# Moving the stores of V, merge gates and gated h to the queues of the engines that make them, V by key and block in DRAM, T blocks on VectorE, and P3 kept in the second quad

## The chip, the cores and the metric

The kernel runs on one core of one Trainium2 chip. The metric is the device time of one execution in microseconds (us). Several runs of a kernel are taken, and their median counts. One more execution is recorded by the hardware profiler; every time of a single instruction, wait or stage below comes from that one, counted from the start of its span.

## The reference, cut to what is computed

One hybrid decoder block, batch 1, 2048 positions, width 1024, float32:

```python
proj = x @ w_in + b_in                      # 1024 -> 9216 columns
q, k, v, g_attn, u_lru, g_lru, gate_logits = split(proj)
q, k = rope(q), rope(k)                     # 3 groups x 8 heads x 64
# group (window, dilation): (128,1), (512,4), (2048,16): causal band attention,
# keys gathered by stride, outputs of the groups weighted by their softmax denominators
attn = merge(dilated_band_attention(q[g], k[g], v[g]) for g in 0, 1, 2)
y_a  = (attn * silu(g_attn)) @ w_attn_proj
u    = causal_depthwise_conv(u_lru)         # width 4
h    = rg_lru(u)                            # gates, then a scan over positions
y_b  = (h * silu(g_lru)) @ w_lru_proj
merged = sigmoid(gate_A) * y_a + sigmoid(gate_B) * y_b
out  = layer_norm(alpha * x + merged @ w_out + b_out)
```

## The kernel before

**Stages.** Stage A (0 to about 1535 us) is the input projection with all that follows elementwise from it; stage B (to about 1900) is attention; stage C1 (to about 2075) merges the groups and projects the LRU branch; stage C2 (to the end) projects the attention branch, merges, projects out and normalises. A float32 product is made of three float32r matmuls: high part times high part, high times low, low times high. So every weight tile and every block of x has a high part (an ACT copy that rounds: `prep_w` L268 for weights, `hi_lo` L220 for x) and a low part (a subtraction: L232 for weights, L221 for x, on VectorE (DVE) or GpSimd (POOL)).

**Stage A.** The positions are in four chunks of 512. A half of the stage takes two chunks; the second half begins at 779.8 us in program order. A *quad* pairs two tiles of 128 output columns with the two chunks of the half and the two halves of the contraction: a 2x2 by 2x2 block product. The first quad of a half computes its 8 block products plainly; the other 35 use a seven-product scheme with the block combinations T1 to T4 of x (in `comb` and `fourth`) and S1 to S4 of the weights (`added`, `sums`). S1 and S3 are made by a DMA that POOL issues and that adds in flight (L250, tile wS). One product is 12 matmuls of 128x512 (L605) into one PSUM bank, and one *tick* of the loop; `evacuate` takes the bank with the seven results kept in part in e, u2 and u3. `MID` and `EDGE` are the orders of the seven products. In the first half the low parts of the weights go to DRAM (L285, `wl_scr`), and the second half loads them back (`load_lo`, L290, tile l, four buffers) in place of computing them; a weight tile comes in 256 KB pieces (L239).

**Chains.** What follows a quad's result is a generator: `qk_chain` (swap of halves by four loads L310, rotary, split, stores L327, L338, L341), `v_chain` (four transposes on PE, ACT copy into the tile vs L366, of which there are two, and the store L370), `mg_chain` (tanh L384, store L390), `silu_chain`, and `lru` (ending with h times its gate on POOL and the store L525 to `hb_scr`). `yield Ask(...)` hands the rest of a chain to a later tick in which the engines named have time left in a budget; `at(tick, fn)` and `later(n, fn)` put work into a fixed tick. The generator only sets the program order of each engine; on the chip each engine runs its own list and waits for semaphores.

**Queues.** SP issues nearly all DMAs; ACT issues the output of attention (L996), the last five stores of `mg_scr` (L386) and the result; POOL issues the accumulating ones. The DMAs of SP and ACT together use eight semaphores in turn (the DMAHW in the order's waits), in program order: each of them waits until the one eight before it has landed. Those of POOL have semaphores of their own (DMASW).

**Attention.** 12 units (`unit_parts`: one head pair of one group, the groups in the order 0, 2, 1) of 16 steps. A unit needs q and k tiles (A from `qh_scr` and `ql_scr` L805, C from `k_scr` L784, split by POOL at L792, L793, L795; L780 and L781 are memsets for the first two units) and the V tile of its group (`v_parts`, L822, L824, L826), which serves four units.

Of the kernel before, what the change touches and what calls it, by code (L numbers as in the profile page):

```python
# [31 lines left out]
def hybrid_block_kernel(ctx: ExitStack, tc: tile.TileContext, a: dict, out: bass.AP):  # L32
# [16 lines left out]
    v_scr = [[dram.tile([S, 260], F32, name=f"v_scr{g}{j}") for j in range(2)] for g in range(3)]  # L49
# [29 lines left out]

    def softplus():  # L80
        lam = lr[:, 7, :]
        t = [cst.tile([P, 8], F32, name=f"spt{i}") for i in range(4)]
        dve.tensor_scalar(out=t[0], in0=lam, scalar1=-1.0, scalar2=None, op0=ALU.mult)
        dve.tensor_tensor(out=t[1], in0=lam, in1=t[0], op=ALU.min)
        act.activation(t[1], t[1], AF.Exp)
        dve.tensor_scalar(out=t[2], in0=t[1], scalar1=2.0, scalar2=None, op0=ALU.add)
        dve.reciprocal(out=t[2], in_=t[2])
        dve.tensor_tensor(out=t[1], in0=t[1], in1=t[2], op=ALU.mult)
        dve.tensor_tensor(out=t[2], in0=t[1], in1=t[1], op=ALU.mult)
        dve.tensor_scalar(out=t[3], in0=t[2], scalar1=1.0 / 17, scalar2=1.0 / 15, op0=ALU.mult, op1=ALU.add)  # L90
        for c in (13, 11, 9, 7, 5, 3, 1):
            dve.tensor_tensor(out=t[3], in0=t[3], in1=t[2], op=ALU.mult)
            dve.tensor_scalar(out=t[3], in0=t[3], scalar1=1.0 / c, scalar2=None, op0=ALU.add)
        dve.tensor_tensor(out=t[3], in0=t[3], in1=t[1], op=ALU.mult)
        dve.tensor_scalar(out=t[0], in0=t[0], scalar1=0.0, scalar2=2.0, op0=ALU.max, op1=ALU.mult)
        dve.scalar_tensor_tensor(out=sp2, in0=t[3], scalar=4.0, in1=t[0], op0=ALU.mult, op1=ALU.add)
# [39 lines left out]
    MID, EDGE = (1, 6, 7, 5, 2, 4, 3), (1, 2, 6, 7, 4, 5, 3)  # L136
# [91 lines left out]
    def drop_raw(b, kk):  # L228
        give(xr.pop((b, kk)))
# [72 lines left out]
    def qk_chain(rw, f, c):  # L302
# [48 lines left out]
    def v_chain(vt, sgn, f, c):  # L351
# [18 lines left out]
        sp.dma_start(dst.rearrange("(b p) f -> p b f", p=P), vs)  # L370
# [8 lines left out]
    def mg_chain(y, sgn, f, c, bank=None):  # L379
# [50 lines left out]
    def lru(i, c, ub):  # L430
# [91 lines left out]
        tt(pool, g, g, h, ALU.mult)  # L522
        give(h)
        yield Ask()
        sp.dma_start(hb_scr[i * P:(i + 1) * P, c * CH:(c + 1) * CH], g)  # L525
# [13 lines left out]
    for h in range(2):  # L539
        for p, (kind, f0, f1) in enumerate(seq):  # L540
            plan.append((h, ((f0, kind), (f1, kind)), None if p == 0 else EDGE if p == len(seq) - 1 else MID, p, kind))
# [74 lines left out]
    def evacuate(s, j):  # L616
# [20 lines left out]
        elif pid == 5:  # L637
            result(s, 1, c1, b, Q["u3"])
            tt(dve, Q["u2"], Q["u2"], b, ALU.add)
        elif pid == 4:  # L640
            result(s, 1, c0, b, Q["u3"])
        else:
            result(s, 0, c1, b, Q["u2"])
        last = {"e": (2, 6), "u2": (3,), "u3": (4, 5)}
        for n, p in last.items():
            if pid in p and all(order.index(x) <= j for x in p):
# [11 lines left out]
    for s in range(1, NQ):  # L658
# [9 lines left out]
        at(t0 - 4, lambda s=s: added(s, "S1", "A22"))  # L668
        at(t0 - 4, lambda s=s: added(s, "S3", "A11"))
# [29 lines left out]
    def comb(kk):  # L699
# [684 lines left out]
```

## Time and profile before

| | us |
|---|---|
| median of 3 runs | 2354.79 (2354.69 to 2357.52) |
| the profiled execution's own time | 2354.13 |
| its span | 2352.4 |
| PE busy in it | 2241.2 (95%) |
| PE waits for a low-part load in it | 26.8, in 17 waits |
| granted TensorE clock, mean | 0.978 |

The span is what the profiler sees from the first instruction to the last; the execution's own time is 1.7 us longer. The rows of the profile are groups of instructions by line, engine, operation and tile (tile<-inputs), with busy time, the mean duration of one in ns, and the idle time just ahead of them with what ended it. "SPq" is SP's DMA queue; a row of waits has total us, times, longest us. The lines follow where they are used.

### The profile page before, as it was taken

How to read it: one execution, taken by the hardware profiler on the slowest of the kernel's cores; microseconds unless marked ns; L12 is line 12 of the kernel's file. 1: busy time of each engine (PE TensorE's matmuls, PEld its weight loads, DVE VectorE, ACT ScalarE, POOL GpSimd, SP SyncE). 2: the span in 40 equal slices, each digit the busy share in tenths (PEclk: the TensorE clock that was granted, in tenths of full speed). 3: DMA queues.
4: the chain of work that ended last, by engine and by line, in shares of the span. 5: the costliest groups of instructions: out<-in, count | busy, mean ns of one | idle time of the engine just before them, and what ended most of it. 6: DMA issues, size and time to landing. Idle time of an engine off the chain costs nothing.

```text
span 2352.4 us, 34614 instructions
## 1 busy us (share of the span) xinstructions
PE 2241.2 (95%) x11008; PEld 1877.7 (80%) x11008; DVE 1717.5 (73%) x3122; ACT 1087.8 (46%) x1977; POOL 1005.6 (43%) x754
## 2 busy tenths in 40 slices
PE   6999999999999799999999999989999999989998
PEld 4788888888788687787787777788999878768886
DVE  6888888899889676666677776545666568747677
ACT  4346445455455455465465665455666611121100
POOL 5554555456445433223232232357676436612220
PEclk8999999999999899999999999999999999999999
DMA  6887997988988998897898888897786688874431
GB/s 238 246 251 238 278 281 224 281 257 264 268 260 294 287 245 240 243 256 228 236 261 242 260 241 253 255 258 181 196 226 161 175 253 295 267 248 157 157 117 63
DMA packets 347175, 551.48 MB, mean 234 GB/s; under 512 B 99057, under 2 KB 140017, under 8 KB 342385
## 3 DMA queue, kind: packets, MB, share of 16 engines
q1 hardware_dynamic: 308160, 489.80, 66.6%
q0 software_dynamic: 20160, 36.71, 9.6%
q10 hardware_dynamic: 18672, 22.75, 3.1%
q8 instruction: 88, 1.44, 0.3%
q14 instruction: 95, 0.77, 0.1%
HBM read 343.81 MB, written 180.16 MB: 223 GB/s over the span
## 4 chain that ended last, share of the span: by engine, by line
PE 63%; DMA 14%; DVE 8%; issue 6%; POOL 4%; ACT 3%; SPq 2%; ACTq 0%; DVEq 0%; POOLq 0%
PE q L605 44%; DMA l<-wl_scr 4%; PE o L982 3%; DMA A<-qh_scr 2%; PE s L943 2%; PE yb L1171 2%; PE yb L1172 2%; PE yb L1170 2%; PE pt L958 1%; PE z L1264 1%; PE z L1263 1%; PE z L1262 1%; SPq L310 1%; POOL C L795 1%; POOL me L1236 1%
## 5 line engine op out<-in xcount | busy, mean ns | idle before, releaser
L605 PE MATMUL q<-xT,hS 128*128 128x512 f32 x1680 | 523.7, 393 | 8.7 <-ACT hS L268 5.9
L605 PE MATMUL q<-xT,l 128*128 128x512 f32 x1120 | 438.9, 392 | 1.9 <-DVE l L232 1.9
L605 PE MATMUL q<-xB,hA 128*128 128x512 f32 x1248 | 396.2, 399 | 18.4 <-ACT hA L268 10.8
L605 PE MATMUL q<-xB,l 128*128 128x512 f32 x904 | 360.9, 399 | 35.5 <-DMA l<-wl_scr 26.8
L605 PEld LDWEIGHTS q<-xT,hS 128*128 128x128 f32 x1680 | 317.2, 189 | 77.1 <-ACT hS L268 7.1
L605 PEld LDWEIGHTS q<-xB,hA 128*128 128x128 f32 x1248 | 238.8, 193 | 69.0 <-ACT hA L268 11.2
L605 PEld LDWEIGHTS q<-xT,l 128*128 128x128 f32 x1120 | 211.9, 189 | 47.5 <-DVE l L232 3.0
L605 PEld LDWEIGHTS q<-xB,l 128*128 128x128 f32 x904 | 173.2, 192 | 80.3 <-DMA l<-wl_scr 34.6
L949 ACT ACTIVATE p<-p,osb 128x256 f32<-128x256 f32 (+1 forms) x384 | 156.4, 454 | 117.3 <-DVE osb L947 116.7
L232 POOL TENSOR_TENSOR sw<-sw,sin 128x512 f32<-128x512 f32 x96 | 157.9, 1664 | 97.9 <-DMA sw<-y 88.4
L947 DVE CUSTOM_DVE_ANT_0 p<-s,mask 128x256 f32<-128x256 f32 (+1 forms) x384 | 125.3, 364 | 101.5 <-PE s L943 65.5
L250 POOL DMA_DIRECT2D wS<-in_w_in_dram x140 | 123.6, 987 | 168.7 <-DMA wS<-in_w_in_dram 125.5
L268 ACT ACTIVATE hA<-wA 128x512 fp32r<-128x512 f32 x218 | 134.8, 623 | 100.9 <-DMA wA<-in_w_in_dram 50.7
L605 PE MATMUL q<-xB,hS 128*128 128x512 f32 x560 | 175.2, 394 | 2.8 <-DVE v L232 2.8
L605 PE MATMUL q<-xT,hA 128*128 128x512 f32 x560 | 174.1, 392 | 0.2 <-DVE u L232 0.2
L982 PE MATMUL o<-V,ptb 128*128 128x65 f32 x1200 | 165.9, 277 | 7.3 <-ACT ptb L963 5.0
L232 POOL TENSOR_TENSOR S<-S,wA 128x512 f32<-128x512 f32 x35 | 50.3, 1438 | 278.6 <-DVE S L232 96.5
L982 PEld LDWEIGHTS o<-V,ptb 128*128 128x128 f32 x1200 | 153.2, 196 | 18.5 <-ACT ptb L963 16.1
L232 DVE TENSOR_TENSOR y<-y,cos 128x512 f32<-128x512 f32 x96 | 119.3, 1246 | 45.1 <-DMA sw<-y 45.0
L232 POOL TENSOR_TENSOR l<-wA,hA 128x512 fp32r<-128x512 f32 x74 | 117.2, 1584 | 55.8 <-ACT hA L268 37.8
L1236 POOL TENSOR_TENSOR me<-gA,ybr 128x512 f32<-128x512 f32 x32 | 47.1, 1487 | 187.2 <-DVE gA L1235 184.0
L943 PE MATMUL s<-B,A 128*128 128x256 f32 (+1 forms) x384 | 118.2, 329 | 8.8 <-DMA A<-qh_scr 6.9
(193 smaller groups left out, 4970.3 us busy)
## 6 DMA issues: line engine op xcount, KB each, us to landing
wA<-in_w_in_dram SPq DMA_DIRECT2D x218, 256.0 KB, 5.4
wl_scr<-l SPq DMA_DIRECT2D x105, 512.0 KB, 5.0
l<-wl_scr SPq DMA_DIRECT2D x105, 512.0 KB, 6.1
wS<-in_w_in_dram SPq DMA_DIRECT2D x140, 256.0 KB, 5.0
wS<-in_w_in_dram POOLq DMA_DIRECT2D x140, 256.0 KB, 6.9
sw<-y SPq DMA_DIRECT2D x384, 64.0 KB, 3.7
mg_scr<-y SPq DMA_DIRECT2D x59, 256.0 KB, 6.0
o_scr<-osb ACTq DMA_DIRECT2D x48, 264.0 KB, 5.6
```

What stands on the lines that cost most here:

```text
L232: eng.tensor_tensor(out=out, in0=in0, in1=in1, op=op)
L250: pool.dma_start(t, w_part(s, x), accum_op=ALU.add)
L268: act.activation(h, r, AF.Copy)
L605: pe.matmul(bank, w[:, ks], x[:, kk, xx], start=(first and i == 0), stop=(last and i == 11))
L943: pe.matmul(s[:, h, (0 if g == 2 and n else lo):256], q, k, start=(i == 0), stop=(i == 1))
L947: dve.tensor_tensor_reduce(out=p[:, h, lo:256], in0=s[:, h, lo:256], in1=mask[:, lo:256], scale=1.0, scalar=3e38, op0=ALU.add, op1=ALU.min ...
L949: act.activation(p[:, h, lo:256], p[:, h, lo:256], AF.Exp, scale=-1.0, bias=mm)
L982: pe.matmul(o[:, n % 2, h * 65:h * 65 + 65], ptb[:, 2 * h + x, :], V[:, kb, vo + h * 65:vo + h * 65 + 65], start=(x == lo // P), stop=(x = ...
L1170: pe.matmul(yb, WL[f][:, 0, k], xx[:, 0], start=(k == 0), stop=False)
L1171: pe.matmul(yb, WL[f][:, 0, k], xx[:, 1], start=False, stop=False)
L1172: pe.matmul(yb, WL[f][:, 1, k], xx[:, 0], start=False, stop=(k == 7))
L1236: pool.tensor_tensor(out=ME[c][:, f], in0=ga, in1=yb, op=ALU.add)
```

## The change

The code, cut to its core:

```diff
-    v_scr = [[dram.tile([S, 260], F32, name=f"v_scr{g}{j}") for j in range(2)] for g in range(3)]
+    v_scr = [[dram.tile([P, 16, 260], F32, name=f"v_scr{g}{j}") for j in range(2)] for g in range(3)]
...
-    MID, EDGE = (1, 6, 7, 5, 2, 4, 3), (1, 2, 6, 7, 4, 5, 3)
+    MID, EDGE, FIRST = (1, 6, 7, 5, 2, 4, 3), (1, 2, 6, 7, 4, 5, 3), (1, 2, 3, 6, 7, 5, 4)
...
         if not isq:
-            yield Ask()
+            yield Ask(lag=2)
             sp.dma_start(qk_scr["k", u][:, c * CH:(c + 1) * CH], flat(rp))
...
         act.activation(vs[:, :, 1:129], st["tp"], AF.Copy, scale=sgn)
         tog["n"] -= 1
+        fs = slice((hp % 2) * 130, (hp % 2) * 130 + 130)
+        dst = v_scr[g][hp // 2]
+        if g == 0:
+            act.dma_start(dst[:, 4 * c:4 * c + 4, fs], vs)
+        else:
+            n = 4 if g == 1 else 16
+            w = P // n
+            for b in range(4):
+                rows = dst[w * b:w * b + w, 4 * c:4 * c + 4, fs] if g == 1 else dst[32 * c + w * b:32 * c + w * b + w, :, fs]
+                act.dma_start(rows, vs[:, b])
         yield Ask()
-        dst = v_scr[g][hp // 2][c * CH:(c + 1) * CH, (hp % 2) * 130:(hp % 2) * 130 + 130]
-        sp.dma_start(dst.rearrange("(b p) f -> p b f", p=P), vs)
         vs_free.append(vs)
...
         act.activation(y, y if bank is None else bank, AF.Tanh, scale=0.5 * sgn, bias=bh[:, f:f + 1])
-        if now["n"] >= base[NQ - 1]:
-            act.dma_start(mg_scr[i * P:(i + 1) * P, c * CH:(c + 1) * CH], y)
-            give(y)
-            return
+        act.dma_start(mg_scr[i * P:(i + 1) * P, c * CH:(c + 1) * CH], y)
         yield Ask()
-        sp.dma_start(mg_scr[i * P:(i + 1) * P, c * CH:(c + 1) * CH], y)
         give_sent(y)
...
         tt(pool, g, g, h, ALU.mult)
+        pool.dma_start(hb_scr[i * P:(i + 1) * P, c * CH:(c + 1) * CH], g)
         give(h)
         yield Ask()
-        sp.dma_start(hb_scr[i * P:(i + 1) * P, c * CH:(c + 1) * CH], g)
         give_sent(g)
...
-            ... EDGE if p == len(seq) - 1 else MID, p, kind))
+            ... EDGE if p == len(seq) - 1 else FIRST if p == 1 else MID, p, kind))
...
         elif pid == 5:
             result(s, 1, c1, b, Q["u3"])
             tt(dve, Q["u2"], Q["u2"], b, ALU.add)
+            if "p3" in Q:
+                result(s, 0, c1, Q["p3"], Q["u2"])
...
+        elif order.index(5) > j:
+            Q["p3"] = take(f"p{s}", F32)
+            act.activation(Q["p3"], b, AF.Copy)
...
-        at(t0 - 4, lambda s=s: added(s, "S1", "A22"))
-        at(t0 - 4, lambda s=s: added(s, "S3", "A11"))
+        for n, x in (("S1", "A22"), ("S3", "A11")):
+            at(max(t0 - 4, 2), lambda s=s, n=n, x=x: added(s, n, x))
...
         tt(dve, r12, r22, r12, ALU.subtract)
-        hi_lo("T1", kk, r11, pool)
-        tt(dve, r21, r11, r21, ALU.subtract)
-        hi_lo("T3", kk, r12, pool)
-        tt(dve, r11, r11, r22, ALU.add)
-        hi_lo("T2", kk, r11, dve)
-        tt(dve, r21, r21, r22, ALU.add)
+        tt(dve, r22, r11, r22, ALU.add)
+        tt(dve, r21, r22, r21, ALU.subtract)
+        for n, r in (("T2", r22), ("T3", r12), ("T1", r11)):
+            hi_lo(n, kk, r)
...
-        hi_lo("T4", kk, xr["cB21", kk], some(kk))
+        hi_lo("T4", kk, xr["cB21", kk])
...
-        at(E0 + 6 + kk, lambda kk=kk: comb_loads(2, kk))
-        at(E0 + 9 + kk, lambda kk=kk: comb(kk))
+        at(E0 + 4 + kk, lambda kk=kk: comb_loads(2, kk))
+        at(E0 + 7 + kk, lambda kk=kk: comb(kk))
...
-                        pool.memset(flat(B2[u][up_, 0]), 0.0)
-                        pool.memset(flat(B2[u][lo_, 1]), 0.0)
+                        eng = dve if u else pool
+                        eng.memset(flat(B2[u][up_, 0]), 0.0)
+                        eng.memset(flat(B2[u][lo_, 1]), 0.0)
...
-                V = VT[g, j]
-                if g == 0:
-                    sp.dma_start(V[:, 4 * i:4 * i + 4], src[i * CH:(i + 1) * CH].rearrange("(n p) f -> p n f", p=P))
...
-                    sp.dma_start(V[:, 4 * i:4 * i + 4], src.rearrange("(i r) f -> i r f", r=16)[:, 4 * i:4 * i + 4])
+                sp.dma_start(VT[g, j][:, 4 * i:4 * i + 4], src[:, 4 * i:4 * i + 4])
...
-    at(0, lambda: comb_loads(0, 0))
-    at(1, lambda: comb_loads(0, 1))
-    at(2, lambda: comb_loads(0, 2))
-    at(3, lambda: comb_loads(0, 3))
+    for b in ("B11", "B21", "B12", "B22"):
+        for kk in K4:
+            xr["c" + b, kk] = xr[b, kk]
...
-            for fn in ((), (), first[:2], first[2:], firstv, second[:1], second[1:2])[j]:
+            for fn in ((), (), first[:2], first[2:], firstv[:1], second[:1], second[1:2] + firstv[1:2])[j]:
...
-    for fn in second[2:] + v_parts(2, 0):
+    for fn in firstv[2:] + second[2:]:
         fn()
-    VORD = {0: (1, 0), 4: (0, 1), 5: (2, 1), 6: (1, 1)}
-    loads = []
+    VORD = {1: (1, 0), 4: (0, 1), 5: (2, 1), 6: (1, 1)}
+    loads = v_parts(2, 0)
...
-            load_h(c + 1, f)
+            for k in ((0, 1), (2,), (3,), (4,), (5,), (6,), (7,), ())[f]:
+                load_h(c + 1, k)
```

In words. (1) A V tile's store is issued by ACT right behind the copy that makes it, as one DMA in group 0 and as four in groups 1 and 2; `v_scr` is laid out as attention reads it, so each of the 24 loads of V takes 4160 bytes in a row from each partition, where it took pieces of 1040. (2) All 64 stores of the merge gates are issued by ACT behind their tanh. (3) The 32 stores of gated h are issued by POOL behind their product. (4) A store of k stands one tick later. (5) The second quad of each half takes product 3 third, keeps it in a tile p3, and makes its result at product 5. (6) The low parts of T1 to T4 are all DVE's; `comb` adds in another order; in the first half it works on the raw x blocks that are there already, and its 16 loads (4 MB) go; the accumulating DMAs of quad 1 and the splits of B12 and B22 are put into other ticks, as is `comb` with its loads at the half switch. (7) The scales of the LRU (`softplus`) become a chain. (8) In attention the V parts, the parts of unit 1 and the memsets are interleaved differently, and V of group 1 is loaded a unit later. (9) In C1 the loads of h for the next chunk stand one job earlier.

PE's own order keeps its 7378 rows; only the second quads and `comb`'s neighbours differ. Three places show what moves.

SP in the second half at 950 us: l2_45 is a load of low parts for quad 45, y49_2 a gated h, y1_3 a q or k result. Before:

```order
L290 DMA l0_45_9048<-wl_scr9_125 128x1024 [waits DMAHW7_49,PE_49]
L525 DMA hb_scr_71<-y49_2_8686 128x512 [waits DMAHW0_49,Pool_49]
L310 DMA sw1_3_9077<-y1_3_9057 32x512 [waits DMAHW1_49,DVE_49,Activation_49]
L310 DMA sw1_3_9077<-y1_3_9057 32x512 [waits DMAHW2_49]
L310 DMA sw1_3_9077<-y1_3_9057 32x512 [waits DMAHW3_49]
L310 DMA sw1_3_9077<-y1_3_9057 32x512 [waits DMAHW4_49]
L290 DMA l2_45_9099<-wl_scr9_125 128x1024 [waits DMAHW5_49,PE_49]
```

The same place after the change:

```order
L274 DMA l0_45_9060<-wl_scr9_125 128x1024 [waits DMAHW0_49,PE_49]
L294 DMA sw1_3_9090<-y1_3_9070 32x512 [waits DMAHW2_49,DVE_49,Activation_49]
L294 DMA sw1_3_9090<-y1_3_9070 32x512 [waits DMAHW3_49]
L294 DMA sw1_3_9090<-y1_3_9070 32x512 [waits DMAHW4_49]
L294 DMA sw1_3_9090<-y1_3_9070 32x512 [waits DMAHW6_49]
L274 DMA l2_45_9112<-wl_scr9_125 128x1024 [waits DMAHW7_49,PE_49]
```

The store of gated h, and its wait for POOL, is gone from SP; the swap behind it waits for DVE in both, and the gaps in DMAHW1 and DMAHW5 are DMAs that ACT now issues in between.

ACT in the first half, where it makes a V quad of group 1 (vs_202 and vs_203 are the two vs tiles, hA and hS high parts of weights, e the first bank of a quad, hi the high part of a q). After the change:

```order
L350 ACTIVATE vs_202<-vtp_1_2222 128x4x128
L361 DMA v_scr_76<-vs_202 32x4x130 x4
L616 ACTIVATE e_2281<-q_10_2247 128x512
L252 ACTIVATE hA_10_2296<-wA_10_2073 128x512
L316 ACTIVATE hi_1_2302<-y_1_1945 128x512
L350 ACTIVATE vs_203<-vtp_0_2254 128x4x128
L361 DMA v_scr_76<-vs_203 32x4x130 x4
L252 ACTIVATE hS_10_2330<-S_10_2138 128x512
```

Four DMAs stand between an ACT copy and the bank and high parts behind it, where none stood before.

POOL at the start (wS_1 are the raw S1 and S3 of quad 1, l_0 a low part of quad 0, xB the low parts of x). Before:

```order
L221 TENSOR_TENSOR xB_287<-xB_232,xB_287 128x512
L221 TENSOR_TENSOR xB_287<-xB_236,xB_287 128x512
L250 DMA wS_1_304<-in_w_in_dram 128x512
L250 DMA wS_1_306<-in_w_in_dram 128x512
L232 TENSOR_TENSOR l_0_326<-wA_0_238,hA_0_324 128x512
L221 TENSOR_TENSOR xB_358<-xB_244,xB_358 128x512
```

After the change:

```order
L203 TENSOR_TENSOR xB_287<-xB_236,xB_287 128x512
L216 TENSOR_TENSOR l_0_316<-wA_0_238,hA_0_314 128x512
L203 TENSOR_TENSOR xB_318<-xB_244,xB_318 128x512
L203 TENSOR_TENSOR xB_318<-xB_248,xB_318 128x512
L203 TENSOR_TENSOR xB_350<-xB_252,xB_350 128x512
L203 TENSOR_TENSOR xB_350<-xB_256,xB_350 128x512
L234 DMA wS_1_296<-in_w_in_dram 128x512
L234 DMA wS_1_298<-in_w_in_dram 128x512
```

The two accumulating DMAs have moved from ahead of quad 0's low part to behind the splits of B12 and B22.

More of the change, by code (lines that the diff above doesn't have):

```diff
@@ L228, in drop_raw @@
     def drop_raw(b, kk):
-        give(xr.pop((b, kk)))
+        t = xr.pop((b, kk))
+        if xr.get(("c" + b, kk)) is not t:
+            give(t)
     def tt(eng, out, in0, in1, op):
@@ L718, in fourth @@
             new_block("T4")
-        hi_lo("T4", kk, xr["cB21", kk], some(kk))
+        hi_lo("T4", kk, xr["cB21", kk])
         drop_raw("cB21", kk)
-        spend(ACT=.66, DVE=.36, POOL=.7)
+        spend(ACT=.66, DVE=.72)
     K4 = range(4)
@@ L870, in hybrid_block_kernel @@
             at(max(t, 0), fn)
+    for kk in K4:
+        at(3 + kk, lambda kk=kk: comb(kk))
+    at(8, lambda: [fourth(kk) for kk in K4])
+    at(10, lambda: start_chain(scales()))
     first, second, firstv = unit_parts(0), unit_parts(1), v_parts(0, 0)
```

58 lines of the change are left out of this document (27 added, 31 removed).

## The prediction

> **What bounds the kernel now.** I read the busy shares first, then the stages, then what PE waits for, then the queues behind those waits.
>
> From the page and the windows by stage (PE, PEld, DVE, ACT, POOL busy, granted clock, DMA share, GB/s):
>
> ```profile
> PE 2241.2 (95%) x11008; PEld 1877.7 (80%) x11008; DVE 1717.5 (73%) x3122; ACT 1087.8 (46%) x1977; POOL 1005.6 (43%) x754
> 80.00:740.00 660.00, 658.70 (x2946) 543.80 (x2945) 580.34 (x688) 326.39 (x546) 348.06 (x256) 1.00 0.88 260
> 800.00:1200.00 400.00, 385.71 (x1710) 315.73 (x1709) 265.28 (x359) 216.21 (x358) 115.60 (x93) 0.98 0.87 246
> 1200.00:1535.00 335.00, 322.47 (x1393) 263.60 (x1392) 233.72 (x311) 194.74 (x314) 102.75 (x81) 0.98 0.87 252
> ```
>
> PE bounds everything: 95%, and in 80 to 740 us it is idle 1.3 us of 660. No edit of queues can gain there, and PE's own work stays (same rows in the order). A matmul takes 660/2946 = 0.224 us at full clock, a product of 12 takes 2.69 us, a quad of seven 18.8 us. What can be had lies in PE's idle stretches: the start, the half switch, the second half (about 27 of 735 us idle), attention and the merge. PE's waits, total us, times, longest (three rows of it; those of the start and of attention stand at their places):
>
> ```profile
> PE q L605 <- DMA l<-wl_scr: 26.8, 17, 3.4
> PE q L605 <- ACT hA L268: 10.8, 1, 10.8
> PE yb L1170 <- ACT h L1007: 3.2, 1, 3.2
> ```
>
> So I sum over five places, each with what is late next.
>
> **1. The start: -14 us (-18 to -6).** POOL, then PE, in order of time; a window (the clock is the third number from the end); from the list of DMA issues the us to landing of the accumulating ones; DVE's adds for the T blocks in 0 to 80 us (busy, mean ns, idle before and why) and one of them alone:
>
> ```profile
> 21.13 1.90 POOL L250 DMA_DIRECT2D wS<-in_w_in_dram x2 [7.73 <-DMA wS<-in_w_in_dram]
> 24.37 0.80 PE L605 MATMUL q<-xB,l 128*128 128x512 f32 x1 [8.49 <-POOL l L232]
> 49.63 1.22 PE L605 MATMUL q<-xT,hS 128*128 128x512 f32 x2 [3.98 <-ACT hS L268]
> 75.82 0.84 PE L605 MATMUL q<-xB,hS 128*128 128x512 f32 x2 [2.42 <-DVE v L232]
> 80.24 0.62 PE L605 MATMUL q<-xB,hA 128*128 128x512 f32 x2
> 24.30:30.00 5.70, 5.63 (x16) 4.52 (x17) 0.00 (x0) 0.00 (x0) 5.70 (x7) 0.64 1.09 300
> wS<-in_w_in_dram POOLq DMA_DIRECT2D x140, 256.0 KB, 6.9
> L232 DVE TENSOR_TENSOR xcB<-xcB,xcB 128x512 f32<-128x512 f32 x20 | 19.8, 1010 | 11.7 <-POOL xT L221 11.6
> 769.60 0.69 DVE L232 TENSOR_TENSOR xcB<-xcB,xcB 128x512 f32<-128x512 f32 x1 [2.69 <-DMA xcB<-in_xT_dram]
> ```
>
> POOL stood 7.73 us before its accumulating DMA, and quad 0's low part stood behind it on POOL; that cost PE 8.49 us and a clock of 0.64 for the next 5.7 us, some 2 us more. With the DMAs moved behind the splits (the order shows it) PE runs on from 15.9: six products of quad 0 and the three of quad 1 that need no T (FIRST takes product 3 early) are 9 x 2.69 = 24 us, to about 40. Then the T blocks are late. A piece of `comb` is 4 adds and 3 low parts on DVE, 7 x 0.69 = 4.8 us, 19.3 for four. It starts when S1's accumulation has landed, about 28 us (issue at about 21, and 6.9), so the last T2 is there at about 47. Quad 1 has four products left then, 4 x 2.69 = 10.8 us, with 2 us for a low clock after the wait and 4 to 6 for high parts that stand behind ACT's T copies: quad 2, which now begins at 80.24 (the row of 75.82 is the last product ahead of it), begins at 64 to 66. I take 66, -14; -18 if ACT's copies are never late; -6 if only the 8.5 us go and the rest waits for DVE, which now has POOL's share of the low parts too. DVE has room for it: it stood 11.6 us here, for POOL's low parts.
>
> **2. The half switch: -8 us (-13 to -2).** DVE's adds of one `comb` piece and of the one two pieces on, and PE:
>
> ```profile
> 779.74 1.74 DVE L232 TENSOR_TENSOR xcB<-xcB,xcB 128x512 f32<-128x512 f32 x1 [1.18 <-POOL xT L221]
> 794.78 1.75 DVE L232 TENSOR_TENSOR xcB<-xcB,xcB 128x512 f32<-128x512 f32 x1 [1.17 <-POOL xT L221]
> 790.93 1.22 PE L605 MATMUL q<-xB,hA 128*128 128x512 f32 x2 [10.78 <-ACT hA L268]
> ```
>
> The same ping-pong: DVE waits for POOL, its next add takes 1.74 in place of 0.69, and two pieces of `comb` take 15.04 us, 7.5 each. PE's high part hA is on ACT behind the T copies of the third piece, hence 10.78 us. With 4.8 us a piece, 3 pieces end 3 x 2.7 = 8.1 us earlier; loads two ticks earlier may add, and a shorter wait costs less clock, as at the start. At worst 2 us go, at best the whole wait and some clock.
>
> **3. The loads of low parts: -12 us (-22 to +10).** This is the place the moved stores are about. SP's waits, SP in order of time, PE and DVE at the same place, the store of V (issue min/median/max in ns), and landings:
>
> ```profile
> SPq L290 <- PE q L605: 72.2, 38, 5.5
> SPq L525 <- POOL y L232: 53.3, 8, 7.5
> SPq L310 <- DVE y L551: 38.9, 22, 7.7
> 957.44 0.32 SPq L525 DMA_DIRECT2D hb_scr<-y  x1
> 958.68 2.42 SPq L310 DMA_DIRECT2D sw<-y  x4
> 961.21 0.53 SPq L290 DMA_DIRECT2D l<-wl_scr  x1
> 976.48 0.50 PE L605 MATMUL q<-xB,l 128*128 128x512 f32 x1 [0.68 <-DMA l<-wl_scr]
> 957.88 0.74 DVE L551 SCALAR_TENSOR_TENSOR y<-q,bn,v 128x512 f32<-128x512 f32 x1
> L370 SPq DMA_DIRECT2D v_scr<-vs x48: 370/384/1159, 138.5 to 1183.9; - x48
> l<-wl_scr SPq DMA_DIRECT2D x105, 512.0 KB, 6.1
> sw<-y SPq DMA_DIRECT2D x384, 64.0 KB, 3.7
> v_scr<-vs SPq DMA_DIRECT2D x48, 260.0 KB, 4.8
> ```
>
> Eight times SP stands up to 7.5 us before the store of gated h, and PE's waits for l follow; after the hold that ends at 957 the first is at 976.48. But the hold does not go with that store: the swap right behind it needs DVE's y, which ends at 957.88 + 0.74 = 958.62, and began at 958.68. The wait of 53.3 turns mostly into a wait for DVE. What remains is issue: 48 x 0.384 + 59 x 0.33 + 32 x 0.33 = 48 us of SP's time in stage A, and up to ten of those stores stand between such a hold and the last load of a quad, 3.5 us. PE's 17 waits are 1.6 us on average. For gated h and gates, and V in group 0, that clears most; for V in groups 1 and 2 four DMAs take the place of one in the shared ring of eight, where a load issues only when the DMA eight ahead has landed. I take -12, about half of 26.8; -22 if five waits are all that stay; +10 if the extra DMAs lengthen the ring in half of the eight V quads.
>
> V's store on ACT: its issue is near the 0.338 us of ACT's own stores (below), 144 of them are 49 us on an engine busy 54% in 800 to 1200; a hold there is hidden as long as high parts are ready ahead. The trace shows such holds already:
>
> ```profile
> ACT vs L366 <- DMA v_scr<-vs: 37.2, 10, 6.8
> L250 POOL DMA_DIRECT2D wS<-in_w_in_dram x140 | 123.6, 987 | 168.7 <-DMA wS<-in_w_in_dram 125.5
> L996 ACTq DMA_DIRECT2D o_scr<-osb x48: 326/338/421, 1559.3 to 1877.5; - x48
> ```
>
> Ten holds in 800 to 1200 us, to 6.8 us, and PE has no wait for a high part from ACT there. So I cost it at nothing, and +17 a V quad if the cover goes (last rival). Gated h on POOL costs its issue there, by the nearest row (L250, 987 ns) 32 x 0.99 = 32 us of an engine busy 30% in the second half: nothing. k a tick later and the scales in pieces: no reader waits in stage A: nothing, at most 1 us either way.
>
> **4. Into attention: -11 us (-15 to -4).** SP and POOL in order of time, then windows of L943 alone: units 1, 2, 4 and 5 (64 matmuls each):
>
> ```profile
> 1537.12 11.84 SPq L822 DMA_DIRECT2D V<-v_scr  x4
> 1558.69 1.03 POOL L792 CAST B<-C 64x1024 fp32r<-64x1024 f32 x1 [10.36 <-DMA C<-k_scr]
> 1572.20:1601.00 28.80, 12.64 (x64) 9.36 (x64) 0.88 0.88 248
> 1601.00:1634.80 33.80, 13.57 (x64) 10.77 (x64) 0.85 0.58 150
> 1664.40:1686.70 22.30, 11.53 (x64) 8.66 (x64) 1.00 0.95 224
> 1686.70:1712.50 25.80, 11.19 (x64) 8.57 (x64) 1.00 1.03 297
> ```
>
> Units 1 and 2 take 28.8 and 33.8 us where the same groups later take 22.3 and 25.8: 14.5 us too many. The cause is one block: four V loads hold SP 11.84 us, so the k loads of unit 1 come late and POOL's splits stand 10.36 us. With V interleaved and the memsets on DVE the splits start that much earlier; V of group 1 a unit later leaves room for unit 2's loads. I take three quarters, -11; the rest is ring waits behind attention's own stores. Loads of V in long pieces can only be shorter (nothing to -2, within the range).
>
> **5. The merge: -3 us (-4 to +1).** The 3.2 us for h are a load one job too late; it now has one job more. The rest of stage C is not touched.
>
> **Sum.** -14 - 8 - 12 - 11 - 3 = -48. The profiled execution took 2354.13 us (span 2352.4), 0.7 under the median of the runs, so 2306 against it and **2307** as a median.
>
> **Rivals.**
> (B) *The transfers, not the issues, are the limit.* DMA is 0.87 busy in the second half, and a load lands 6.1 us after its issue whoever issues the rest; then earlier issues land no earlier and term 3 is nothing: 2319. For it: share and landing. Against: PE's waits follow SP's holds. The Trainium skill, "DMA: Bandwidth & Descriptors", section "Issuing engines are not separate DMA queues", says the same: DMAs of several engines share the 16 DMA engines, and issuing from more engines saves only sequencer time, usually small beside the transfer. By it the sum is 2319; the share of 0.87 agrees, the holds on SP speak against it.
> (C) *The ring fills.* 12 more DMAs in each of four V quads of the second half, each in the ring for some 3.7 us (the 64 KB row) over eight places: 12 x 3.7/8 = 5.6 us a quad, 22 in all, in place of term 3: 2307 + 12 + 22 = 2341 at most, 2331 with half hidden. For it: every load passes that ring. The Trainium skill, same page, section "Rules for kernel authors", wants many small transfers made into one large; the rows agree in that a fourth of the bytes takes 3.7 in place of 4.8 us.
> (D) *T blocks stay late.* ACT's copies, or DVE (88% busy), set the pace and terms 1 and 2 give 4 in place of 22: 2325.
> (E) *Slower: ACT is held in each V burst.* Place: v quads of groups 1 and 2. ACT has 18.8 x 46% = 8.6 us free a quad, four bursts in it; it decides when a burst holds ACT over 8.6/4 = 2.2 us. A burst that waits a landing and issues four, 4.8 + 4 x 0.38 = 6.3 us, makes 25 - 8.6 = 17 us a quad, 132 for eight; at two thirds of the hold 66. With term 3 lost: 2385 to 2450. Against it: the ten holds that cost PE nothing.
> (F) *Nothing moves*, since PE's waits are only pushed on: 2353.
>
> **How the numbers follow.** Forecast 52%, its own range 2293 to 2318; B 13%; C 12%; D 8%; E 12%; F 1%; better than 2286 2%. The range reaches from 2286 to 2338: it leaves out E, F, the best 2% and a quarter of C, 18%. A measurement of this kernel tells some 0.2% (4.7 us) from no change. Faster: all but E, F and a quarter of C, 84%; same 4%; slower 12%.
>
> **What would show it.** Right: POOL's wait of 7.73 and PE's of 8.49 gone and quad 2 begun at 64 to 66, not 80.24; the wait for hA at 5 or less; PE's waits for l at 10 to 15; SP's wait for POOL replaced by one for DVE's y; units 1 and 2 under 25 and 29 us; no PE wait for an ACT high part in 860 to 1200. Wrong: waits of PE for hA or hS in V quads (E), waits for l above 26 with ACT's queue in SP's way (C), hA at the half switch as before (D).

## The result and the profile after

The changed kernel takes 2358.94 us in the median of 20 runs (2347.18 to 2368.61), the kernel before on the same chips 2356.1 (2349.6 to 2367.02): a ratio of 1.0007, 95% interval 0.9991 to 1.0023. Nothing was gained or lost. The forecast was 2307 and its range ended at 2338. The profiled execution of after is one of the slower ones, 2365.78 us with a span of 2364.0, against 2354.13 and 2352.4 of before, so its stages add up to 11.6 us more.

The windows of the page's stages in after (PE, PEld, DVE, ACT, POOL busy, clock, DMA share, GB/s), to be laid beside those of before:

```profile
0.00:80.00 80.00, 67.80 (x264) 52.56 (x265) 61.29 (x91) 39.85 (x68) 39.63 (x37) 0.96 0.73 231
80.00:740.00 660.00, 640.75 (x2834) 524.94 (x2833) 564.84 (x683) 320.22 (x532) 333.70 (x259) 0.99 0.86 252
800.00:1200.00 400.00, 383.28 (x1691) 311.96 (x1690) 256.25 (x347) 212.34 (x354) 114.86 (x98) 0.98 0.85 241
1200.00:1535.00 335.00, 318.95 (x1366) 259.37 (x1366) 242.33 (x320) 194.99 (x313) 106.25 (x91) 0.98 0.87 251
```

The second row is the surprise: PE did 2946 matmuls in 80 to 740 us and was idle 1.3 us; now it does 2834 and is idle 19.2. What PE waits for in after, over the whole span:

```profile
PE q L593 <- DMA l<-wl_scr: 31.7, 20, 4.5
PE q L593 <- ACT hA L252: 15.8, 6, 12.0
PE o L987 <- ACT ptb L968: 12.3, 17, 6.8
PE q L593 <- DVE u L216: 4.6, 6, 1.7
PE q L593 <- DVE v L216: 4.5, 4, 2.7
PE vtp L342 <- DVE y L539: 4.2, 3, 1.9
PE q L593 <- DVE y L539: 3.6, 1, 3.6
```

The wait for POOL's l of 8.5 us is gone. But the loads l cost more than before (31.7 for 26.8), hA at the half switch is as long (12.0 for 10.8), and there are new waits for DVE in the first half: for u, v and y at L593, where a product finds its PSUM bank not yet emptied, and at L342, where the transposes of a v wait for the y that DVE makes.

Since PE takes its products in the same order in all kernels here but for the second quads, a stage can be cut by PE's own matmuls, not by the clock on the wall. This table has the start of quad 2, quad 36 (the first of the second half) and quad 38, the last product of stage A and the span, in us, and then what each of the five stretches took more or less than in before. Two profiles of one kernel need not agree: in e11, where the first half is that of before, its stretch is 6.5 us longer, so a difference below that in one of the two halves tells nothing by itself. The start and the switch repeat better (-0.1 and +0.8 in e11).

| kernel | quad 2 | 36 | 38 | end of A | span | start | first half | switch | second half | rest |
|---|---|---|---|---|---|---|---|---|---|---|
| before | 80.2 | 758.2 | 816.4 | 1543.6 | 2352.4 | | | | | |
| after | 61.0 | 765.0 | 821.8 | 1557.3 | 2364.0 | -19.2 | +26.0 | -1.3 | +8.3 | -2.1 |
| e1, V back | 61.2 | 752.9 | 809.2 | 1539.1 | 2338.2 | -19.0 | +13.7 | -1.9 | +2.7 | -9.6 |
| e2, gates back | 60.9 | 760.3 | 810.8 | 1544.5 | 2348.9 | -19.4 | +21.4 | -7.7 | +6.5 | -4.3 |
| e3, gated h back | 61.4 | 759.2 | 818.4 | 1560.4 | 2354.3 | -18.8 | +19.7 | +1.1 | +14.8 | -14.8 |
| e4, all three back | 61.1 | 741.3 | 792.3 | 1522.1 | 2326.9 | -19.1 | +2.2 | -7.2 | +2.6 | -4.0 |
| e5, e4 and V on ACT, one DMA | 61.2 | 742.0 | 793.1 | 1520.5 | 2321.7 | -19.1 | +2.8 | -7.1 | +0.2 | -7.5 |
| e6, e4 and V on SP, four, new layout | 61.0 | 754.1 | 804.8 | 1544.0 | 2340.3 | -19.3 | +15.1 | -7.5 | +12.0 | -12.5 |
| e7, e4 and l a tick earlier | 60.9 | 741.5 | 792.1 | 1506.5 | 2310.6 | -19.3 | +2.6 | -7.6 | -12.8 | -4.7 |
| e8, e4 and T1, T3 on POOL | 68.0 | 750.3 | 805.1 | 1529.1 | 2330.1 | -12.3 | +4.4 | -3.4 | -3.2 | -7.7 |
| e9, e4 and gates on ACT | 61.1 | 746.9 | 805.4 | 1538.5 | 2341.9 | -19.2 | +7.9 | +0.3 | +5.9 | -5.3 |
| e10, e4 and gated h on POOL | 60.3 | 751.1 | 802.5 | 1530.0 | 2335.4 | -19.9 | +12.8 | -6.8 | +0.3 | -3.3 |
| e11, before and l a tick earlier | 80.1 | 764.7 | 823.6 | 1533.4 | 2347.4 | -0.1 | +6.5 | +0.8 | -17.4 | +5.3 |
| e12, e4 and V on SP, four, old layout | 60.9 | 747.7 | 798.5 | 1533.2 | 2337.3 | -19.4 | +8.9 | -7.5 | +7.6 | -4.7 |
| e13, e4 and V on POOL, four, new layout | 60.4 | 749.0 | 800.2 | 1522.7 | 2322.1 | -19.9 | +10.7 | -7.0 | -4.7 | -9.4 |
| e14, e4 and attention's old order | 61.0 | 744.2 | 796.3 | 1525.4 | 2329.5 | -19.2 | +5.2 | -6.1 | +1.9 | -4.6 |
| e15, e5 and l a tick earlier | 60.4 | 741.6 | 791.6 | 1503.0 | 2299.3 | -19.9 | +3.2 | -8.2 | -15.8 | -12.5 |
| e16, e13 and l a tick earlier | 60.6 | 746.4 | 796.7 | 1504.7 | 2301.4 | -19.6 | +7.8 | -8.0 | -19.1 | -12.1 |

So the start gave 19 us, more than forecast, and the first half, which had no term in the sum, took 26 back. Of these PE is idle for 18.3 (19.6 us between quad 2 and quad 36, 1.3 before); in the other 7.7 the same matmuls take longer, at a mean granted clock of 0.99 where before has 1.00.

**A first theory.** ACT's row in after's first V quad of group 1 shows what stands where the high parts should come. ACT, in order of time:

```profile
235.71 3.94 ACTq L361 DMA_DIRECT2D v_scr<-vs  x4
239.70 0.63 ACT L252 ACTIVATE hS<-S 128x512 fp32r<-128x512 f32 x1 [4.51 <-DMA v_scr<-vs]
...
241.37 2.66 ACTq L361 DMA_DIRECT2D v_scr<-vs  x4
244.13 0.63 ACT L252 ACTIVATE hS<-S 128x512 fp32r<-128x512 f32 x1 [2.79 <-DMA v_scr<-vs]
...
245.95 2.51 ACTq L361 DMA_DIRECT2D v_scr<-vs  x4
```

DVE and PE in the same quad, a little later:

```profile
252.92 5.38 DVE L216 TENSOR_TENSOR y<-y,cos 128x512 f32<-128x512 f32 x1
258.22 0.74 DVE L539 SCALAR_TENSOR_TENSOR y<-q,b,u 128x512 f32<-128x512 f32 x1
259.10 1.19 PE L593 MATMUL q<-xT,hS 128*128 128x512 f32 x2 [3.61 <-DVE y L539]
```

A burst of four takes 2.5 to 3.9 us; it delays a high part, POOL's work behind it bunches, a DVE product of 0.69 us lasts 5.38 beside that, and PE finds its bank full. That is theory A: V's stores on ACT hold the high parts. (Products and additions of over 4 us are in the kernel before too, five of them for three in after, so they alone are not what the change added.) Against it stood B (gated h on POOL), C (T blocks and ticks) and D (merge gates on ACT).

### The profile page after: what moved, and what is told of

It is laid out like the page before. It is cut to its first block, busy times and chain, and to the rows that moved or that the text cites. A ratio compares the mean times of both kernels' runs of the same rounds, so it can differ in the third digit from the quotient of the medians.

```text
span 2364.0 us, 34586 instructions
## 1 busy us (share of the span) xinstructions
PE 2245.4 (95%) x11008; PEld 1877.1 (79%) x11008; DVE 1718.4 (73%) x3136; ACT 1090.8 (46%) x1979; POOL 983.1 (42%) x764
## 3 DMA queue, kind: packets, MB, share of 16 engines
q1 hardware_dynamic: 264336, 448.96, 61.1%
## 5 line engine op out<-in xcount | busy, mean ns | idle before, releaser
L593 PE MATMUL q<-xT,hS 128*128 128x512 f32 x1680 | 521.2, 391 | 4.9 <-DVE y L539 3.6
L593 PE MATMUL q<-xT,l 128*128 128x512 f32 x1120 | 437.9, 391 | 0.6 <-DMA l<-wl_scr 0.6
L593 PE MATMUL q<-xB,hA 128*128 128x512 f32 x1248 | 395.3, 398 | 20.3 <-ACT hA L252 13.7
L593 PE MATMUL q<-xB,l 128*128 128x512 f32 x904 | 362.7, 401 | 33.5 <-DMA l<-wl_scr 31.1
L593 PEld LDWEIGHTS q<-xT,hS 128*128 128x128 f32 x1680 | 316.0, 189 | 71.7 <-issue 4.9
L593 PEld LDWEIGHTS q<-xB,hA 128*128 128x128 f32 x1248 | 237.6, 192 | 72.7 <-ACT hA L252 15.7
L593 PEld LDWEIGHTS q<-xT,l 128*128 128x128 f32 x1120 | 211.1, 189 | 45.8 <-DMA l<-wl_scr 1.5
L593 PEld LDWEIGHTS q<-xB,l 128*128 128x128 f32 x904 | 174.1, 193 | 81.2 <-DMA l<-wl_scr 40.7
L593 PE MATMUL q<-xB,hS 128*128 128x512 f32 x560 | 179.9, 403 | 7.3 <-DVE v L216 4.5
L216 POOL TENSOR_TENSOR sw<-sw,sin 128x512 f32<-128x512 f32 x96 | 148.5, 1551 | 86.4 <-DMA sw<-y 55.6
L987 PE MATMUL o<-V,ptb 128*128 128x65 f32 x1200 | 165.0, 275 | 15.3 <-ACT ptb L968 12.3
L593 PE MATMUL q<-xT,hA 128*128 128x512 f32 x560 | 174.0, 392 | 5.6 <-DVE u L216 4.4
L216 DVE TENSOR_TENSOR y<-y,cos 128x512 f32<-128x512 f32 x96 | 113.4, 1185 | 43.4 <-DMA sw<-y 43.2
L252 ACT ACTIVATE hS<-S 128x512 fp32r<-128x512 f32 x140 | 87.4, 624 | 98.2 <-DVE S L216 48.6
L593 PEld LDWEIGHTS q<-xB,hS 128*128 128x128 f32 x560 | 106.7, 194 | 31.0 <-issue 6.5
```

The source lines that it names most:

```text
L216: eng.tensor_tensor(out=out, in0=in0, in1=in1, op=op)
L252: act.activation(h, r, AF.Copy)
L593: pe.matmul(bank, w[:, ks], x[:, kk, xx], start=(first and i == 0), stop=(last and i == 11))
L987: pe.matmul(o[:, n % 2, h * 65:h * 65 + 65], ptb[:, 2 * h + x, :], V[:, kb, vo + h * 65:vo + h * 65 + 65], start=(x == lo // P), stop=(x = ...
```

## The experiments

Each ratio is to the kernel before on the same chip, with its 95% interval. "Back" means as in the kernel before.

**e1 to e4: one kind of store back, then all three.** The edits of e2 and e3; e1 puts `v_scr`, V's store and its loads back as the diff above has them with -; e4 is the three together.

```diff
-        act.dma_start(mg_scr[...], y)
-        yield Ask()
+        yield Ask()
+        sp.dma_start(mg_scr[...], y)          # e2, the last quad as before
...
-        pool.dma_start(hb_scr[...], g)
-        give(h)
-        yield Ask()
+        give(h)
+        yield Ask()
+        sp.dma_start(hb_scr[...], g)          # e3
```

> The changed kernel with V alone put back: its stores from SP, a tick later, one DMA each, old layout and old loads. Theory A (the bursts of V stores hold ACT, the high parts behind them come late, DVE and POOL slip, PE waits for its banks): the 26 us lost between quad 2 and quad 36 of the first half come back, 2330 to 2338 us, and the gain of 19 at the start is still there at quad 36. Theory B (gated h on POOL is the cost): no change, 2355 to 2362. Theory C (the T blocks and the new ticks are the cost): no change, 2355 to 2362. Theory D (merge gates on ACT): no change, 2355 to 2362.

> The changed kernel with the stores of the merge gates alone put back on SP. Theory A: one store a gate holds ACT little, within 5 us of the changed kernel, 2354 to 2362. Theory B and C: the same. Theory D: 2335 or less.

> The changed kernel with the stores of gated h alone put back on SP. Theory A, C and D: within 5 us of the changed kernel, 2354 to 2362. Theory B: 2335 or less, and fewer long additions on DVE beside POOL's stores.

> The changed kernel with all three kinds of stores put back on SP (V in its old layout), so that the T blocks on DVE, the second quad's order, the start, attention's order and the earlier loads of h stand alone. Theory A, B or D: the gains of start (-19), attention (-2 to -6) and merge (-3) without the loss, 2325 to 2335. Theory C: 2350 to 2360.

Measured: e1 0.9923 (0.9897 to 0.9949), e2 0.9969 (0.9952 to 0.9987), e3 0.9983 (0.9962 to 1.0004), e4 0.9852 (0.9825 to 0.9879). C falls: without the three moved kinds of store the rest of the change gains 35 us. No single one of A, B and D holds alone: V takes some 20 us (1.0007 - 0.9923), the gates 9, gated h 6 with an interval that reaches nothing. Theory A came near with its price (e1 2340.33 us for 2330 to 2338), but only 12 of the 26 us of the first half come back with V. D's and B's 2335 did not come. e4's first half is whole again (+2.2), and its loads of l are no better for it: 28.7 us in 19 waits.

**e5, e6 and e12: what it is about V's stores.** All on e4.

```diff
-        yield Ask()
         dst = v_scr[g][hp // 2][c * CH:(c + 1) * CH, ...]
-        sp.dma_start(dst.rearrange("(b p) f -> p b f", p=P), vs)
+        act.dma_start(dst.rearrange("(b p) f -> p b f", p=P), vs)   # e5: ACT, one DMA
+        yield Ask()
...
+            for b in range(4):                                      # e6: SP, new layout
+                sp.dma_start(rows, vs[:, b])
...
+            for b in range(4):                                      # e12: SP, old layout
+                sp.dma_start(dst[b * P:b * P + P], vs[:, b])
```

> The kernel with all stores on SP, but V's stores from ACT right behind the copy, one DMA each in the old layout (48 DMAs on ACT in place of 144). Theory A1 (it is the number of issues: a burst of four takes ACT 2.5 us at least, 4 x 0.62): near the kernel with all stores on SP, ratio to before 0.984 to 0.988. Theory A2 (it is the queue: ACT then waits for SP's DMAs in the shared ring): half or more of the loss is there, ratio 0.990 to 0.994.

> The kernel with all stores on SP, V's stores from SP too, but in the new layout: four DMAs in groups 1 and 2, and long pieces in attention's loads. Theory A1 and A2: what cost was ACT's time, so stage A stays within 4 us of the kernel with all stores on SP, and attention may gain 0 to 3: ratio 0.983 to 0.987. Rival (96 more DMAs fill the ring): PE's waits for l rise from 28.7 to 40 or more, ratio 0.990 or more.

> The kernel with all stores on SP and V in the old layout, with the one store of a V tile in groups 1 and 2 cut into four, a block each. Theory N (it is the number of DMAs, in SP's time and in the ring of eight): as slow as with four in the new layout up to the end of stage A, ratio 0.993 to 0.998. Theory P (it is the pattern of the new layout): ratio 0.984 to 0.988.

Measured: e5 0.9874 (0.9856 to 0.9892), e6 0.9961 (0.9946 to 0.9976), e12 0.9951 (0.9930 to 0.9973). That turns theory A: ACT as the issuer costs nothing that these intervals show beside e4, and four DMAs a tile cost 23 to 26 us (0.0099 and 0.0109 of 2356) on SP too, in either layout. It is the count. Two expected signs did not come: PE's waits for l in e6 are 34.4 us and not 40, and up to the end of stage A e12 loses 11 us against e4 where e6 loses 22; e6 has some of that back in the rest. e6 shows where the count bites on SP; SP in order of time:

```profile
409.55 2.92 SPq L362 DMA_DIRECT2D v_scr<-vs  x4
412.56 2.90 SPq L294 DMA_DIRECT2D sw<-y  x4
415.56 2.13 SPq L362 DMA_DIRECT2D v_scr<-vs  x4
418.50 2.41 SPq L294 DMA_DIRECT2D sw<-y  x4
```

The same place in e4, with one store a tile:

```profile
399.99 0.39 SPq L354 DMA_DIRECT2D v_scr<-vs  x1
400.47 3.41 SPq L294 DMA_DIRECT2D sw<-y  x4
404.08 0.43 SPq L354 DMA_DIRECT2D v_scr<-vs  x1
405.50 2.91 SPq L294 DMA_DIRECT2D sw<-y  x4
```

And in e6 behind it, DVE and then PE:

```profile
419.32 0.69 DVE L216 TENSOR_TENSOR y<-y,cos 128x512 f32<-128x512 f32 x1 [7.23 <-DMA sw<-y]
431.01 1.19 PE L597 MATMUL q<-xT,hA 128*128 128x512 f32 x2 [3.99 <-DVE u L216]
```

The same product of DVE in e4, behind which PE does not wait:

```profile
407.39 0.69 DVE L216 TENSOR_TENSOR y<-y,cos 128x512 f32<-128x512 f32 x1 [1.23 <-DMA sw<-y]
```

Each tile takes 2 us more of SP's list, the swaps behind it land late, DVE, which works in order, stands 7.23 us for one, and PE waits 3.99 us for the bank behind that. On ACT the same burst stands before high parts: another victim, and in e1 about the same price (20 us). That the high parts carry it there is read from the rows of the first theory; no run tried four stores on ACT on e4.

**e13: the ring, or the issues.** e6 with `pool.dma_start(rows, vs[:, b])`, in group 0 still SP.

> The kernel with all stores on SP, but V in the new layout with its four stores a tile from POOL, whose DMAs have semaphores of their own and pass neither SP's list nor the ring of eight. Theory R (the ring of eight and SP's list are the place of the loss): most of the 25 us come back up to the end of stage A, ratio 0.984 to 0.989. Theory I (128 issues cost whatever engine makes them, since the issuer's own work behind them is late): 128 x 0.6 us on POOL, its rotary products late, DVE behind them, ratio 0.992 or more.

Measured: 0.9857 (0.9841 to 0.9874), theory R's number: POOL makes the same 128 issues, outside SP's list and the ring of eight, and the 25 us are back. Its stages say it less cleanly. The second half is 16.7 us shorter than e6's, the first half only 4.4, and 8.5 longer than e4's; with single profiles 6.5 us apart, whether POOL's issues cost something in the first half stays open. No run parts the ring itself from the time in SP's list. The traces speak for the list: summed over the first half, SP issues for 33 us longer in e6 than in e4 (445 for 412) and waits 6 us longer for DMAs to land (28 for 22).

**e9 and e10: gates on ACT and gated h on POOL, each alone on e4** (the lines of the change).

> The kernel with all stores on SP, and the 59 stores of the merge gates on ACT behind their tanh as in the change. Theory M1 (a queue's place does not matter, as V's one DMA on ACT showed: 0.9874 beside 0.9852): ratio 0.984 to 0.988. Theory M2 (the store leaves ACT's tanh before the ring is free, and ACT waits with the high parts behind it): 5 to 10 us lost, ratio 0.988 to 0.991, with PE waiting for DVE's u, v or for ACT's hA in the quads of the gates.

> The kernel with all stores on SP, and the 32 stores of gated h on POOL behind their product as in the change. Theory H1 (0.61 us of POOL each, off the path): ratio 0.984 to 0.988. Theory H2 (POOL's issue holds up POOL's additions and DVE's beside them, and SP's wait only turns from POOL to DVE, so nothing is gained): 5 to 10 us lost, ratio 0.988 to 0.991, SP's wait for POOL gone, its wait for DVE's y above 70, PE's waits for l at 25 or more.

Measured: e9 0.9911 (0.9881 to 0.9941), e10 0.9880 (0.9846 to 0.9914). The gates on ACT cost 14 us beside e4, M2 and a little more, and the place that the table shows is the half switch (7.5 us); the halves differ by 5.7 and 3.3, less than two profiles do. ACT of e9 at the switch:

```profile
781.27 0.33 ACTq L369 DMA_DIRECT2D mg_scr<-y  x1
781.64 0.69 ACT L368 ACTIVATE y<-q,bh 128x512 f32<-128x512 f32 x1 [0.40 <-ACT y L368]
786.30 0.33 ACTq L369 DMA_DIRECT2D mg_scr<-y  x1
786.68 0.63 ACT L252 ACTIVATE hA<-wA 128x512 fp32r<-128x512 f32 x1 [4.35 <-DMA mg_scr<-y]
```

PE of e9, then PE of e4, at the half switch:

```profile
780.68 1.22 PE L585 MATMUL q<-xB,hA 128*128 128x512 f32 x2 [11.65 <-ACT hA L252]
787.36 0.96 PE L585 MATMUL q<-xB,hA 128*128 128x512 f32 x2 [2.00 <-ACT hA L252]
```

```profile
770.26 1.22 PE L589 MATMUL q<-xB,hA 128*128 128x512 f32 x2 [7.08 <-ACT hA L252]
```

The store at 786.30 waits nearly 4 us for its place, and hA stands behind it: PE's second wait, of 2.00. The first wait is 4.6 us longer than e4's, and most of that begins on SP. SP's wait for a gate's store ahead of the loads of x, and DVE's first additions for the T blocks, in e9 and then in e4:

```profile
SPq L208 <- DMA mg_scr<-y: 4.5, 1, 4.5
760.01 2.87 DVE L216 TENSOR_TENSOR xcB<-xcB,xcB 128x512 f32<-128x512 f32 x4 [2.67 <-DMA xcB<-in_xT_dram]
```

```profile
SPq L208 <- DMA mg_scr<-y: 0.4, 1, 0.4
749.82 3.71 DVE L216 TENSOR_TENSOR xcB<-xcB,xcB 128x512 f32<-128x512 f32 x4 [0.17 <-DMA xcB<-in_xT_dram]
```

A store that ACT issues keeps its place in the ring of eight, so a load of SP eight places on waits until the gate has landed. The loads for the T blocks stand behind that load: DVE begins 13.1 us after the start of quad 36 in e9 and 8.5 in e4 (13.0 in after, 8.8 in e2). The two stores straight ahead of hA on ACT add about 1 us. The kernels with all the gates on ACT (after, e1, e3, e9) have -1.9 to +1.1 at the switch, the others with the T blocks on DVE -6.1 to -8.2.

For gated h on POOL e10's 7 us lie where the intervals of e10 and e4 overlap; H2's signs are there (SP's wait for POOL gone, for DVE's y at L294 85.2 us where e4 has 44.8; l at 27.6), so it gained nothing. Its first half is 10.6 us longer than e4's in the one profile, its second half 2.3 shorter; how much it costs stays open.

**e7 and e11: what the loads l wait for.** On e4, and on the kernel before with nothing else changed:

```diff
-                at(t0 + j - 1, lambda s=s, j=j: load_lo(s, j))
+                at(t0 + j - 2, lambda s=s, j=j: load_lo(s, j))
```

> The kernel with all stores on SP, and every load of low parts in the second half one tick (2.7 us) earlier in the order. Theory L1 (the loads come late because the swaps ahead of them on SP wait for DVE): PE's waits for l fall from 28.7 to 12 or less, ratio 0.976 to 0.980. Theory L2 (the buffer is the limit: the load then waits for PE to leave it): l stays above 22, SP's wait for PE rises from 72 to 90 or more, ratio 0.984 to 0.987.

> The kernel before, with nothing changed but every load of low parts in the second half one tick earlier in the order. If PE's waits for l come from the load's place behind the swaps on SP, and not from the stores that the change moved, they fall from 26.8 to 10 or less and the ratio is 0.990 to 0.994. If the loads need the room that the moved stores would leave, the waits stay above 18 and the ratio is 0.996 to 1.002.

Measured: e7 0.9799 (0.9778 to 0.9819), e11 0.9927 (0.9900 to 0.9953). PE's waits in e7, and in e11:

```profile
PE q L589 <- DMA l<-wl_scr: 4.6, 5, 2.1
```

```profile
PE q L605 <- DMA l<-wl_scr: 9.4, 11, 1.5
```

SP's wait for PE to leave the buffer grew from 72 to about 135 us in both, which leaves little for a second tick; none was tried. The loads wanted another place in the list, 17 us in the kernel before, not the room that moved stores leave.

**e8 and e14: the T blocks, and attention's order, each undone on e4.**

```diff
-        for n, r in (("T2", r22), ("T3", r12), ("T1", r11)):
-            hi_lo(n, kk, r)
+        for n, r, e in (("T2", r22, dve), ("T3", r12, pool), ("T1", r11, pool)):
+            hi_lo(n, kk, r, e)                                      # e8
...
-        spend(ACT=2.0, DVE=4.8)
+        spend(ACT=2.0, DVE=3.5, POOL=2.8)                           # e8
...
-    VORD = {1: (1, 0), 4: (0, 1), 5: (2, 1), 6: (1, 1)}
+    VORD = {0: (1, 0), 4: (0, 1), 5: (2, 1), 6: (1, 1)}             # e14, with the rest of part 8
```

> The kernel with all stores on SP, and the low parts of T1 and T3 back on POOL, all else of the start and the half switch as changed. Theory S1 (DVE waiting for POOL was the loss, as predicted): quad 2 begins 6 to 10 us later than 61.1, quad 38 another 4 to 7, ratio 0.989 to 0.993. Theory S2 (the moved accumulating DMAs and the second quad's order made the gain): quad 2 begins within 3 us of 61.1, ratio 0.985 to 0.988.

> The kernel with all stores on SP, with the old order of V's loads, of unit 1's parts and of the memsets (part 8 undone alone). If that part gains what the waits at units 1 and 2 showed: 8 to 11 us slower than with it, ratio 0.988 to 0.990. If the waits only moved on (from k and q to V): within 4 us, ratio 0.984 to 0.987.

Measured: e8 0.9892 (0.9875 to 0.9910), e14 0.9871 (0.9855 to 0.9888). With T1 and T3 on POOL quad 2 begins at 68.0 in place of 61.1, and the switch loses 3.8 of its 7.2 us: S1. The other 12 us of the start stay with the rest of parts 5 and 6 (the moved accumulating DMAs, the second quad's order, the 16 loads that go), which were not parted. e14 is 0.0019, some 4 us, above e4, and the two intervals overlap: no gain of attention's new order is shown, though they do not shut out 8 us. From the end of stage A on the two profiles differ by 0.6 us, so the waits seem only to have moved on.

**e15 and e16: what the runs point to.** e15 is e5 with l a tick earlier; e16 is e13 with it.

> The two that helped together: all stores on SP but V's (one DMA each, on ACT, old layout), and every load of low parts one tick earlier. The parts add: ratio 0.978 to 0.982, PE's waits for l under 10 us. If the load of SP alone decided, V's 48 DMAs off SP give more: 0.976.

> The two repairs that worked, together in the new layout: V's stores, four a tile, from POOL, attention's loads of V in long pieces, all other stores on SP, and every load of low parts one tick earlier. If the repairs add up as with V on ACT: ratio 0.977 to 0.981, PE's waits for l under 10 us. If POOL's 128 issues now show, since DVE and POOL are late in the second half: 0.983 or more.

Measured: e15 0.9789 (0.9769 to 0.9809), 2308.13 us; e16 0.9768 (0.9746 to 0.9790), 2303.40 us, both faster than either kernel. The parts add (e16 ends just under its range). The busy line of e16's page, and PE's wait for l in it:

```profile
PE 2225.1 (97%) x11008; PEld 1863.1 (81%) x11008; DVE 1725.2 (75%) x3136; ACT 1088.3 (47%) x1979; POOL 1038.1 (45%) x860
```

```profile
PE q L597 <- DMA l<-wl_scr: 4.0, 4, 2.3
```

Which of the two is faster their intervals do not tell.

## Why the prediction was wrong

Two steps failed above all: four stores a tile for V were costed at nothing and took some 20 us, and the time taken off SP was to give 12 us and gave none.

**The start (forecast -14): right, and larger.** -19.2 us, past the range's -18; quad 2 begins at 61.0 and not at 66. The 4 to 6 us for high parts behind ACT's T copies were not needed; without them the prediction's own terms come to 59.8. The mechanism holds (e8 for DVE's part of it), the accumulating DMA's own part was not tried alone.

**The half switch (-8): right without the gates on ACT, nothing with them.** e4 has -7.2, after -1.3, e2 (gates back) -7.7. DVE no longer waits for POOL there, as forecast, but even e4's wait for hA is 7.08 us and not 5 or less. The sum took 59 x 0.33 us of issuing off SP for the gates and set nothing against it. It did not ask which of SP's loads stand behind those stores in the ring, nor what stands behind them on ACT, at the one place where PE waits for an ACT tile. SP in after, ahead of the loads for the T blocks:

```profile
SPq L208 <- DMA mg_scr<-y: 6.1, 1, 6.1
```

In after the wait for hA is 12.0 us.

**The loads l (-12): the step that failed in the mechanism.** The prediction saw that the wait of 53.3 would turn into one for DVE's y, and it did; after's SP:

```profile
SPq L294 <- DVE y L539: 96.3, 24, 8.4
SPq L274 <- PE q L593: 88.5, 38, 5.5
```

It then took "that clears most" for the rest, on 48 us of removed issue time. That time was not on the path: l costs 31.7 us with it gone (after) and 28.7 with it back (e4), and between 22.7 (e13) and 38.6 (e3) in all the kernels with the loads in their old place. Nor was it free: summed from quad 2 to the end of stage A, SP issues for 85 us less in after than in before, and waits 105 us longer for DMAs to land (211 for 106). A load stands behind a swap that waits for DVE, and its place in the list decides (e7, e11).

**V's stores on ACT (nothing): the step with the largest error.** "So I cost it at nothing" rested on ten holds of ACT that cost PE nothing. Those were holds in the second half, where the loads bring low parts ready made; in the first half DVE is 88% busy, PE had 1.3 us idle, and a hold there can be passed on to DVE and so to the banks, as the rows of the first theory suggest. Rival C had the right thing, the ring and four DMAs a tile, but only for the second half, at 2331 to 2341 us; rival E had all eight V quads, and ACT as the victim, at 66 to 132 us. What the runs show is C's count with both halves as place: 23 to 26 us in e6 and e12, 20 in e1. The rule that spoke against the change was quoted there: the Trainium skill, "DMA: Bandwidth & Descriptors", section "Rules for kernel authors", would have small transfers made into one. The runs agree where SP issues them (e6, e12), with four stores of 65 KB where one of 260 KB landed in about 5 us; issued by POOL they cost nothing in all (e13). The same page of the Trainium skill, section "Issuing engines are not separate DMA queues", says that the DMAs of several engines share the DMA engines and that a second issuer usually saves little. e5 agrees: no gain from the queue alone. e13 beside e6 does not: there another issuer is worth 25 us.

**Attention (-11) and the merge (-3).** From the end of stage A to the end after gains 2.1 us in its profile, for 14 forecast. Unit 1 now (L948 alone), and below it ACT and PE in order of time:

```profile
1589.00:1620.70 31.70, 12.74 (x65) 9.83 (x65) 0.84 0.79 225
```

```profile
1605.58 0.37 ACTq L1001 DMA_DIRECT2D o_scr<-osb  x1
1606.00 0.40 ACT L954 ACTIVATE p<-p,osb 128x128 f32<-128x128 f32 x1 [7.85 <-DMA o_scr<-osb]
1607.59 1.11 PE L987 MATMUL o<-V,ptb 128*128 128x65 f32 x4 [6.84 <-ACT ptb L968]
```

Unit 2 takes 25.7 us (33.8 before), but unit 1 takes 31.7 (28.8): ACT's own store of o waits for the ring, 7.85 us, and PE behind it 6.84. The prediction had put a quarter aside for "ring waits behind attention's own stores"; they took nearly all, and e14, where no gain of the order shows, does not speak against it. Kernels with V in long pieces have some of the shorter ends in the table (-12.5, -9.4, -12.1), but so have e15 and e1 without them, so that part is open. The merge did what was forecast: from the last product of attention to the last of the LRU branch (1876.8 to 2067.1 us before, 1889.8 to 2077.6 after) 2.5 us came back; the wait of 3.2 for h is gone.

## What to carry to other kernels

A store moved to the engine that makes its data puts its issues and its ring wait in front of everything that engine does next, and where the two queues share a ring, the queue that it left still waits for it. One store a tile of V did no harm there (e5), four did: count the issues, and look for the one place where the bottleneck waits for that engine. Where a hold disappears from a queue, look at what the next entry of the queue waits for; if that is as late, move the entry that is needed, not the one in its way. A stage in which the bottleneck engine has no idle time has a term in the sum as well, and for an edit of queues it can only be a loss.

## What the runs showed of the hardware

A smaller DMA was not issued faster: on ACT a 65 KB store of V took 0.526 us to issue in the median (326 ns to 2.107 us) where a 256 KB store of a gate took 0.326; on POOL the 65 KB store took 0.551. The 96 issues more that four stores a tile make cost 23 to 26 us from SP. A DVE product of 0.69 us lasted up to 6.07 us while POOL ran a row of instructions without a gap, in the kernel before as well (up to 5.58).
